# HGRN2 scores: lags 0 to 3 as elementwise products summed by a ones matrix, the tree from four up in place

## The chip, the cores and the metric

One NeuronCore of one Trainium2 chip runs the whole program. The metric is device time in microseconds, the median of several runs. Engines are named as in the profile: PE is TensorE (matmuls; PEld is its weight load), DVE is VectorE, ACT is ScalarE, POOL is GpSimd, SP is SyncE, which issues the DMAs.

## The reference

One layer of a hybrid decoder step for 256 prompt tokens and 8 x 8 sample tokens (320 in all), model width 2048, all in float32. One input projection feeds two mixers, an mLSTM branch (4 heads) and an HGRN2 branch (8 heads, key width 128, value width 256); their outputs are projected, gated, merged, projected again, and a feed-forward layer of width 8192 follows. What the change touches is the HGRN2 recurrence,

```python
# S_t = diag(f_t) S_{t-1} + (1 - f_t) i_t^T,   o_t = S_t^T q_t, chunkwise:
G = jnp.cumsum(lfc, axis=2)                             # log decay, per key channel
rel = G[:, :, :, None, :] - G[:, :, None, :, :]         # t, s, key
rel = jnp.where(causal[:, :, None], rel, -jnp.inf)
a = jnp.sum(qc[:, :, :, None, :] * jnp.exp(rel) * kc[:, :, None, :, :], axis=-1)
o = einsum('bhts,bhsv->bhtv', a, ic) + einsum('bhtk,bhkv->bhtv', qc * jnp.exp(G), S)
```

that is, a score a[t, s] for each pair s <= t: the sum over the 128 key channels of q_t, k_s and the product of the decays f between s and t. The decay depends on the channel, so the scores are not one matmul of q and k.

## The kernel before

The layout has features on the 128 partitions and the 320 tokens along the free dimension: 256 prompt tokens as two tiles of 128, then 64 sample tokens, eight sequences of eight.

**The stream of projections.** Nearly all matmul work is one stream of 304 output tiles of 128 features, each 16 contraction blocks deep, in the fixed order of `tile_list`. Operands are split into a high and a low fp32r part: ACT rounds the high part, DVE subtracts to get the low part, and three fp32r matmuls 320 wide (high x high, high x low, low x high) stand for one fp32 one. Weights come as half tiles of 128 x 1024 through three raw buffers (`wr`), and are split into three buffer pairs (`wh`, `wl`; `prep`, L465). Each head of HGRN2 follows four weight tiles: `hf`, `hq` and two `hi`, with two gate tiles ahead.

**Who sets the order.** While the program is built, a planner (`Sched`, with chains written as Python generators) keeps an estimated clock for each engine. After the matmuls of each contraction block it advances every side chain whose inputs it believes ready, and only then emits the instruction. So side work of a head is strewn between the projection matmuls, and each engine then executes its own instructions in that emitted order. Costs are given by `act`, `dve`, `pe_f` and `pe_r` and by pools of buffers (`acq`, `rel`); a side matmul is emitted once its input is 450 ns old by the planner's clock (`PE_LAT`) beyond a latency of 140.

**The scores of a head** are built as a tree in `h_scan` and `h_a`. At level B (1, 2, 4, ..., 64) tokens are taken in blocks of 2B; for pairs with s in the left half and t in the right half, the score is the dot product of (k_s times the decays from s to the end of its half) and (q_t times the decays from the start of its half to t). `h_scan` keeps these running factors in `fs` (left in one row, right in the other), multiplies them into q and k at each level (L1297, one product of 320 or 256 elements into a buffer `y`), and extends them by the other half's total (L1302 and L1304). `h_a` multiplies the tiles of `y` on PE in plain fp32, 64 columns for each of three (levels 1, 2, 4, with the sample tokens) or two tiles, and copies the pairs that belong to the level into the score buffer `at` under a mask (L1342). The diagonal is a matmul of q and k times the identity (L1327). Level 128, between the two prompt tiles, is one 128-wide matmul.

`h_state` and `h_update` handle the sample states, `h_sp` the prompt's final state, `h_i` the values, `h_out` the outputs. The masks are loaded at the program's start as int32 and narrowed by POOL.

Of the kernel before, what the change touches and what calls it, by code (L numbers as in the profile page):

```python
# [8 lines left out]
F32 = mybir.dt.float32  # L9
# [18 lines left out]
LEVELS = (1, 2, 4, 8, 16, 32, 64)  # L28
# [50 lines left out]
def constants():  # L79
# [16 lines left out]
    m = np.zeros((128, len(LEVELS), 64), np.int32)  # L96
    for n, b in enumerate(LEVELS):
        right = (i // b) % 2 == 1
        t = i[right]
        m[:, n, :] = (i[:, None] // (2 * b) == t[None, :] // (2 * b)) & ((i[:, None] // b) % 2 == 0)  # L100
# [6 lines left out]
    return c, m.reshape(128, -1), r.reshape(128, 256)  # L107
# [178 lines left out]
class Program:  # L286
    def __init__(self, tc, nc, d, pools):
# [3 lines left out]
        self.lmask = p.tile([128, len(LEVELS) * 64], U8, name="lmask")  # L291
# [12 lines left out]
        self.f2 = p.tile([128, 5280], F32, name="f2")  # L304
# [29 lines left out]
    def carve(self):  # L334
# [42 lines left out]
        self.at = Pool([A(512) for _ in range(2)])  # L377
        self.yb = Pool([A(384) for _ in range(2)])
# [7 lines left out]
        self.hkz0 = self.ra[:, 5376:6400]  # L386
        self.hkst = Pool([self.hkz0.rearrange("p (x g k) -> p x g k", x=4, g=2)])
# [4 lines left out]
        self.sg = Pool([Part(self.f2, 4960)(320), self.tst2])  # L392
# [8 lines left out]
    def carve_h(self):  # L401
        C = self.Part(self.pool.tile([128, 5120], F32, name="f3h", tag="f3"))
        qz = C(256)
        self.hqz = Pool([qz])
        for x in (qz, self.ats0, self.hkz0.bitcast(F32), *(y[64:128, 2, :] for y in self.it2)):
# [7 lines left out]
        self.sg.free += [(now, self.f2[:, 4960:5280]), (now, self.late[0])]  # L413
        self.sr.free.append((now, self.late[1]))
        self.ld = Pool(self.late[2:])
# [134 lines left out]
    def before(self, i, t):  # L550
# [44 lines left out]
    def start(self):  # L595
# [28 lines left out]
        lm = self.f2[:, 0:448].bitcast(I32)  # L624
        self.dma(lm, d["lmask"])
# [8 lines left out]
        nc.gpsimd.tensor_copy(self.lmask, lm)  # L634
# [579 lines left out]
    def h_start(self, h):  # L1214
# [4 lines left out]
        m["qk"], m["fs"], m["iv"] = a.three(2, 384), a.three(2, 320), a.three(2, 320)  # L1219
        for n in ("f", "q", "lv", "o", "pre8", "suf", "I", "SP", "S", "aT", "qz", "ist", "sdone", "got", "ld"):  # L1220
            m[n] = Ev()
        m["i"] = [Ev(), Ev()]
        m["Y"] = [Ev() for _ in range(9)]
        s = self.s
        s.spawn(self.h_scan(h), 4)
        s.spawn(self.h_a(h), 4)
# [21 lines left out]
    def ev_hf(self, h, c, b):  # L1248
        v, m = self.nc.vector, self.hh[h]
        fs, qk = m["fs"], m["qk"]  # L1250
        u = fs[:, 0, :]
        if h < 4:
            yield ("pool", 200, lambda: self.nc.gpsimd.memset(qk[:, :, 320:384], 0.0))
        yield from self.sigmoid(b[:, :TOK], u, fs[:, 1, :], ((self.mbank, b),))
        lb, l1 = self.lbv[:, h:h + 1], self.lbv[:, 8 + h:9 + h]
        yield ("dve", dve(TOK, mode=2), lambda: v.tensor_scalar(fs[:, 1, :], u, l1, lb, ALU.mult, ALU.add))
        yield ("act", act(TOK), lambda: self.A(qk[:, 0, 0:TOK], fs[:, 1, :], AF.Identity, scale=-1.0, bias=self.one))
        yield ("pool", 500, lambda: self.nc.gpsimd.memset(u, 1.0))
        yield post(m["f"])

    def ev_hq(self, h, c, b):
        m = self.hh[h]
        yield ("act", act(TOK, True), lambda: self.A(m["qk"][:, 1, 0:TOK], b[:, :TOK]))
        yield rel(self.mbank, b)
        yield post(m["q"])
# [17 lines left out]
    def h_scan(self, h):  # L1283

        v, m = self.nc.vector, self.hh[h]
        yield wait(m["f"], m["q"], m["got"])
        qk, fs = m["qk"], m["fs"]
        m["y"] = [None] * 9
        for n, B in enumerate(LEVELS + (128,)):
            T = TOK if B < 8 else NP_  # L1290
            y = yield acq(self.yb)
            pat = [[2 * B, T // (2 * B)], [320 + B, 2], [1, B]]
            patq = [[2 * B, T // (2 * B)], [384 + B, 2], [1, B]]
            if B < 8:
                yield ("pool", 150, lambda: self.nc.gpsimd.memset(y[:, 320:384], 0.0))
            yo = y[:, 0:T].rearrange("p (j c i) -> p j c i", c=2, i=B)
            yield ("dve", dve(T), lambda: v.tensor_tensor(yo, cap(qk, 0, patq), cap(fs, 0, pat), ALU.mult))  # L1297
            m["y"][n] = y
            yield post(m["Y"][n])
            half = lambda x, r: cap(fs, 320 * x + B * r, [[2 * B, T // (2 * B)], [1, B]])  # L1300
            tot = lambda r: cap(fs, 320 + B * r + B - 1, [[2 * B, T // (2 * B)], [0, B]])
            yield ("dve", dve(T / 2), lambda: v.tensor_tensor(half(0, 0), half(0, 0), tot(1), ALU.mult))  # L1302
            if B < 128:
                yield ("dve", dve(T / 2), lambda: v.tensor_tensor(half(1, 1), half(1, 1), tot(0), ALU.mult))  # L1304
            if B == 4:
                yield post(m["pre8"])
            if B == 128:

                yield post(m["suf"])

    def h_a(self, h):
        v, m = self.nc.vector, self.hh[h]
        if h:
            yield wait(self.hh[h - 1]["got"])
        yield wait(m["f"], m["q"])
        yield self.mdone()
        qk = m["qk"]
        at = yield acq(self.at)
        m["at"] = at
        yield post(m["got"])  # L1320
        a3 = at[:, 0:384].rearrange("p (a t) -> p a t", a=3)
        b = yield acq(self.sbank)
        for i in range(3):
            c = slice(128 * i, 128 * i + 128)
            yield ("pe", pe_f(128), lambda: self.mm(b[:, c], qk[:, 0, c], qk[:, 1, c], start=True, stop=True))
        idb = self.ident.unsqueeze(1).to_broadcast([128, 3, 128])
        yield ("dve", dve(384, True), lambda: v.tensor_tensor(a3, b[:, 0:384].rearrange("p (a t) -> p a t", a=3), idb, ALU.mult))  # L1327
        yield rel(self.sbank, b)
        for n, B in enumerate(LEVELS):
            yield wait(m["Y"][n])  # L1330
            y = m["y"][n]
            w = 3 if B < 8 else 2
            b = yield acq(self.sbank)
            for i in range(w):
                c = slice(128 * i, 128 * i + 128)
                right = y[:, c].rearrange("p (j c i) -> p j c i", c=2, i=B)[:, :, 1, :]
                yield ("pe", pe_f(64), lambda: self.mm(b[:, 64 * i:64 * i + 64], y[:, c], right, start=True, stop=True))
            yield rel(self.yb, y)
            ar = a3[:, 0:w, :].rearrange("p a (j c i) -> p a j c i", c=2, i=B)[:, :, :, 1, :]
            mk = self.lmask[:, 64 * n:64 * n + 64].unsqueeze(1).to_broadcast([128, w, 64]).rearrange("p a (j i) -> p a j i", i=B)  # L1340
            bv = b[:, 0:64 * w].rearrange("p (a j i) -> p a j i", a=w, i=B)
            yield ("dve", dve(64 * w, True) + (150 if w > 2 else 0), lambda: v.copy_predicated(ar, mk, bv))  # L1342
            yield rel(self.sbank, b)
        yield wait(m["Y"][7])
        y = m["y"][7]
        b = yield acq(self.sbank)
        yield ("pe", pe_f(128), lambda: self.mm(b[:, 0:128], y[:, 0:128], y[:, 128:256], start=True, stop=True))
        yield rel(self.yb, y)
        yield ("act", act(128, True), lambda: self.A(at[:, 384:512], b[:, 0:128]))
        yield rel(self.sbank, b)  # L1350
        yield post(m["aT"])

    def h_i(self, h):
# [17 lines left out]
        yield ("act", act(256, True), lambda: self.A(it[0:64, 2, :], b[64:128, 0:256]))  # L1371
# [30 lines left out]
    def h_state(self, h):  # L1402

        nc, v, m = self.nc, self.nc.vector, self.hh[h]
        if h:
            yield wait(self.hh[h - 1]["S"])
        yield wait(m["pre8"])
        qk, fs = m["qk"], m["fs"]

        qz = yield acq(self.hqz)  # L1410
        sv = lambda x: x[:, 256:320].rearrange("p (b t) -> p b t", t=8)
        yield ("dve", dve(64), lambda: v.tensor_tensor(
            cap(qz, 0, [[136, 2], [32, 4], [1, 8]]), by_token(qk[:, 1, :], 256, False), by_token(fs[:, 1, :], 256, False), ALU.mult))
        sm = yield acq(self.sm)
        yield ("dve", 80, lambda: v.tensor_copy(sm[:, 0:8], sv(fs[:, 1, :])[:, :, 7]))
        ks = fs[:, 0, 256:320]
        yield ("dve", dve(64), lambda: v.tensor_tensor(ks, qk[:, 0, 256:320], ks, ALU.mult))
# [20 lines left out]
        for g in range(2):  # L1438
            e = Ev()
            ends.append(e)  # L1440
            self.s.spawn(self.h_update(h, g, m["sb"][g], kst, sm, e), 5)
# [11 lines left out]
        yield rel(self.sm, sm)  # L1453
# [18 lines left out]
    def h_sp(self, h):  # L1472
# [5 lines left out]
        qk, fs, it = m["qk"], m["fs"], m["it"]  # L1478
        ks = fs[:, 0, 0:256]
        yield ("dve", dve(256), lambda: v.tensor_tensor(ks, qk[:, 0, 0:256], ks, ALU.mult))  # L1480
# [452 lines left out]
```

## Time and profile before

| | |
|---|---|
| median of 3 runs | 2347.54 us (2347.39 to 2348.0) |
| profiled execution, first to last instruction (span) | 2342.5 us; no other time of it is recorded, 5.0 us under the median of the runs |
| PE busy | 2331.8 us, 15956 matmul records |
| DVE, ACT, POOL busy | 1363.1, 1055.6, 15.6 us |
| HBM read, written | 371.57 MB, 50.90 MB |
| granted TensorE clock, mean | 0.998 |

A profile row names the line, the engine, the operation, output and input by the program's buffer names, the shape (partitions x elements) and a count; then busy time and the mean duration of one. A plain-fp32 matmul leaves two records, an fp32r one leaves one. Matmuls are pipelined and each record reaches into the next, so the busy column of PE is no price; differences between starts are.

### The profile page before, as it was taken

Reading aid. Unit: us, or ns where it says so; the run is one execution under the profiler, and the core shown is the slowest. Engines: PE = TensorE matmul, PEld = TensorE weight load, DVE = VectorE, ACT = ScalarE, POOL = GpSimd, SP = SyncE. Lnnn points to the kernel's source line nnn. Section 1 sums busy time; section 2 is a strip of 40 time slices with the busy share of each in tenths; the row PEclk is TensorE's granted clock in tenths of the full one; section 3 lists DMA queues with packets and bytes.
Section 4 is the critical chain, followed back from the end, with each engine's and each line's share of the span. In section 5 each row is a group of like instructions: output and inputs, shape, how many; then the busy total and the mean of one; then the engine's idle time right before and its main releaser. Section 6 shows DMA issues by size and latency. Waiting matters only on the chain.

```text
span 2342.5 us, 39167 instructions
## 1 busy us (share of the span) xinstructions
PE 2331.8 (100%) x15956; PEld 2289.7 (98%) x15956; DVE 1363.1 (58%) x2296; ACT 1055.6 (45%) x1685; POOL 15.6 (1%) x65
## 2 busy tenths in 40 slices
PE   9999999999999999999999999999999999999998
PEld 8999999999999999999999999999999999999998
DVE  5565566677666676555555766544554455445555
ACT  4444445445555565444433545533442344234434
POOL 0000000000000000000000000000000000000000
PEclk9999999999999999999999999999999999999999
DMA  7576857655554554545545644444444444444465
GB/s 247 195 259 209 285 189 271 231 182 209 171 180 171 178 188 169 181 170 175 176 168 177 222 166 144 145 152 152 145 147 151 152 145 152 146 153 144 153 225 180
DMA packets 145628, 425.03 MB, mean 181 GB/s; under 512 B 18468, under 2 KB 39972, under 8 KB 144424
## 3 DMA queue, kind: packets, MB, share of 16 engines
q1 hardware_dynamic: 143864, 415.72, 51.5%
q0 software_dynamic: 1152, 6.29, 0.8%
q8 instruction: 124, 2.03, 0.4%
q10 hardware_dynamic: 432, 0.52, 0.1%
q14 instruction: 56, 0.46, 0.1%
HBM read 371.57 MB, written 50.90 MB: 180 GB/s over the span
## 4 chain that ended last, share of the span: by engine, by line
PE 98%; DVE 1%; DMA 0%; ACT 0%; SPq 0%; issue 0%; DVEq 0%
PE bank L328 97%; DMA f<-xT 0%; DVE f3m L1827 0%; DVE f3m L1822 0%; PE bank L1534 0%; PE bank L917 0%; PE bank L1143 0%; PE bank L1365 0%; PE bank L1423 0%; PE bank L1370 0%; PE bank L990 0%; PE bank L1483 0%; PE bank L964 0%; DVE xl L673 0%; ACT xh L322 0%; SPq L331 0%
## 5 line engine op out<-in xcount | busy, mean ns | idle before, releaser
L465 DVE TENSOR_TENSOR wl<-wr,wh 128x1024 fp32r<-128x1024 f32 x428 | 524.4, 1225 | 477.4 <-ACT wh L322 473.4
L328 PE MATMUL bank<-xh,wh 128*128 128x320 f32 (+1 forms) x2432 | 794.8, 327 | 1.7 <-ACT xh L322 1.5
L328 PE MATMUL bank<-xh,wl 128*128 128x320 f32 (+1 forms) x2432 | 755.0, 310 | 0.0
L328 PE MATMUL bank<-xl,wh 128*128 128x320 f32 (+1 forms) x2432 | 753.6, 310 | 1.3 <-DVE xl L673 1.3
L322 ACT ACTIVATE wh<-wr 128x1024 fp32r<-128x1024 f32 (+1 forms) x431 | 453.7, 1053 | 436.6 <-PE bank L328 418.5
L328 PEld LDWEIGHTS bank<-xh,wh 128*128 128x128 f32 x2432 | 460.3, 189 | 20.5 <-issue 15.5
L328 PEld LDWEIGHTS bank<-xl,wh 128*128 128x128 f32 x2432 | 460.7, 189 | 4.7 <-DVE xl L673 1.9
L328 PEld LDWEIGHTS bank<-xh,wl 128*128 128x128 f32 x2432 | 459.4, 189 | 0.0
L465 DVE TENSOR_TENSOR bb<-wr,bb 128x1024 fp32r<-128x1024 f32 x179 | 219.4, 1226 | 236.1 <-ACT bb L322 236.1
L328 PE MATMUL bank<-xh,bb 128*128 128x322 f32 x1280 | 287.2, 311 | 0.0
L328 PE MATMUL bank<-ra,bb 128*128 128x320 f32 x1264 | 284.0, 309 | 0.0
L322 ACT ACTIVATE bb<-wr 128x1024 fp32r<-128x1024 f32 x179 | 188.8, 1055 | 208.2 <-PE bank L328 197.9
L328 PE MATMUL bank<-rxb,bb 128*128 128x320 f32 x1112 | 255.4, 310 | 0.0
L328 PE MATMUL bank<-ra,wh 128*128 128x320 f32 x892 | 250.2, 309 | 0.0
L328 PEld LDWEIGHTS bank<-xh,bb 128*128 128x128 f32 x1280 | 216.0, 188 | 0.0
L328 PEld LDWEIGHTS bank<-ra,bb 128*128 128x128 f32 x1264 | 210.7, 188 | 0.4
L328 PE MATMUL bank<-xl,bb 128*128 128x322 f32 x640 | 198.9, 311 | 0.0
L328 PEld LDWEIGHTS bank<-rxb,bb 128*128 128x128 f32 x1112 | 188.3, 188 | 0.2
L322 ACT ACTIVATE f<-f,misc 128x320 f32<-128x320 f32 x210 | 118.1, 562 | 148.9 <-DVE f L1790 137.2
L328 PE MATMUL bank<-rxb,wh 128*128 128x320 f32 x596 | 184.5, 310 | 0.0
L328 PE MATMUL bank<-rxb,wl 128*128 128x320 f32 x596 | 184.1, 309 | 0.0
L328 PEld LDWEIGHTS bank<-ra,wh 128*128 128x128 f32 x892 | 161.6, 188 | 1.1 <-DVE ra L1564 1.0
(246 smaller groups left out, 2274.2 us busy)
## 6 DMA issues: line engine op xcount, KB each, us to landing
wr<-wt SPq DMA_DIRECT2D x607, 512.0 KB, 3.3
rx<-C SPq DMA_DIRECT2D x34, 256.0 KB, 4.9
Cs<-rx SPq DMA_DIRECT2D x34, 256.0 KB, 4.4
f<-C SPq DMA_DIRECT2D x30, 256.0 KB, 5.0
Cs<-f SPq DMA_DIRECT2D x30, 256.0 KB, 4.4
vD<-ra SPq DMA_DIRECT2D x4, 1024.0 KB, 7.4
f<-S SPq DMA_DIRECT2D x8, 512.0 KB, 6.1
f3h<-S SPq DMA_DIRECT2D x8, 512.0 KB, 6.0
```

The source lines that it names most:

```text
L322: return self.nc.scalar.activation(out, in_, func, **kw)
L328: self.nc.tensor.matmul(*a, **kw)
L465: self.V().tensor_tensor(lo, raw, hi.bitcast(F32), ALU.subtract)
```

## The change

A head's scores are built in another way; everything else stays.

- **Lags 0 to 3** (s = t - d within a block of four tokens) no longer go through the tree. DVE multiplies q, shifted by d, with k into a buffer `P`: 320, 240, 160 and 80 products for d = 0, 1, 2, 3, that is 800 columns; between lags q is multiplied by the decay, so after the last one q holds its factor for the level of four. `P` is split into a high and a low fp32r part (ACT, then DVE), and PE sums over the 128 channels with a matrix of ones as the stationary operand: four fp32r matmuls, 480 and 320 wide for each part. Every row of the result then holds the sums, and masked copies put them on the diagonals of `at` (`h_lag`), which POOL has filled with zeros.
- **The tree begins at four** and works in place: k and q themselves carry the factors, the totals of the blocks lie in small buffers `t[2]` to `t[128]`, and there are no buffers `fs` and `y` and no products into them.
- **Levels 32 and 64** take both prompt tiles in one matmul 128 wide: ACT gathers the left halves of both tiles into a buffer `yk`, and small ACT copies place the blocks of the result into `at` (`h_put`). Levels 4, 8 and 16 stay with a matmul for each tile and a masked copy.
- `h_a` is gone; the placing runs in chains of its own (`put`). The next head's scan waits for this head's `sc`. The state chains read k and q directly (one DVE product for the sample queries becomes an ACT copy; two DVE products and a small copy go).
- The masks are bytes from the host, loaded when the first `mk` tile starts, without the narrowing by POOL. Some buffers move or shrink (`at` 512 to 496, `f2` 5280 to 5232).

```diff
-LEVELS = (1, 2, 4, 8, 16, 32, 64)
+LEVELS = (8, 16)
+M_LAG = (0, 320, 560, 720)
+M_4, M_8, M_END = 800, 960, 960 + 64 * len(LEVELS)
...
         elif kind == "mk" and h == 0 and c == 0:
             self.load_ev.t = s.t["pe"]
+            self.dma(self.lmask, self.d["lmask"])
...
     def h_scan(self, h):
-        yield wait(m["f"], m["q"], m["got"])
-        for n, B in enumerate(LEVELS + (128,)):
-            T = TOK if B < 8 else NP_
-            y = yield acq(self.yb)
...
-            yield ("dve", dve(T), lambda: v.tensor_tensor(yo, cap(qk, 0, patq), cap(fs, 0, pat), ALU.mult))
...
-            yield ("dve", dve(T / 2), lambda: v.tensor_tensor(half(0, 0), half(0, 0), tot(1), ALU.mult))
+        if h:
+            yield wait(self.hh[h - 1]["sc"])
+        yield wait(m["fd"], m["qd"])
+        k, q, f, t = m["k"], m["q"], m["f"], m["t"]
+        P = yield acq(self.pb)
...
+        for d in range(4):
+            n = 80 * (4 - d)
...
+            p = place(P, d).rearrange("p (b r) -> p b r", r=4 - d)
+            yield ("dve", dve(n), lambda: v.tensor_tensor(p, qr[:, :, d:4], kr[:, :, 0:4 - d], ALU.mult))
+            yield ("dve", dve(n), lambda: v.tensor_tensor(qr[:, :, d:4], qr[:, :, d:4], fr[:, :, 0:4 - d], ALU.mult))
...
+        yield ("act", act(800), lambda: self.A(ph, P))
...
+        yield ("dve", dve(800), lambda: v.tensor_tensor(pl, P, ph.bitcast(F32), ALU.subtract))
...
+        yield ("pool", 500, lambda: nc.gpsimd.memset(at[:, 0:TOK], 0.0))
+        ones = self.ones.bitcast(F32R)
+        b = yield acq(self.sbank, 2)
+        for i, (lo, hi) in enumerate(((0, 480), (480, 800))):
+            for x in range(2):
+                yield ("pe", pe_r(hi - lo), lambda: self.mm(b[i][:, 0:hi - lo], ones, phl[:, x, lo:hi], start=x == 0, stop=x == 1))
+        self.put(h, self.h_lag(b, at))
+        for B in (4, 8, 16, 32, 64, 128):
+            b = yield acq(self.sbank)
+            T = TOK if B == 4 else NP_
+            if B < 32:
+                for n, lo in enumerate((0, 128, 192) if B == 4 else (0, 128)):
+                    w = 32 if n == 2 else 64
...
+                    yield ("pe", pe_f(64), lambda: self.mm(b[:, 64 * n:64 * n + w], k[:, lo:lo + 128], right, start=True, stop=True))
+            elif B < 128:
+                yk = yield acq(self.hyk)
...
+                yield ("act", act(128), lambda: self.A(cap(yk, 0, [[64, 2], [32, 2], [1, 32]] if B == 32 else [[64, 2], [1, 64]]), left))
+                yield ("pe", pe_f(128), lambda: self.mm(b[:, 0:128], yk, right, start=True, stop=True))
+            else:
+                yield ("pe", pe_f(128), lambda: self.mm(b[:, 0:128], k[:, 0:128], q[:, 128:256], start=True, stop=True))
+            self.put(h, self.h_put(b, at, B))
...
+            yield ("dve", dve(T / 2), lambda: v.tensor_tensor(two(k)[:, :, 0, :], two(k)[:, :, 0, :], wide(1), ALU.mult))
             if B < 128:
+                yield ("dve", dve(T / 2), lambda: v.tensor_tensor(two(q)[:, :, 1, :], two(q)[:, :, 1, :], wide(0), ALU.mult))
+                yield ("dve", 90, lambda: v.tensor_tensor(t[2 * B][:, 0:T // (2 * B)], tt[:, :, 0], tt[:, :, 1], ALU.mult))
...
-    def h_a(self, h):
-            for i in range(w):
...
-                yield ("pe", pe_f(64), lambda: self.mm(b[:, 64 * i:64 * i + 64], y[:, c], right, start=True, stop=True))
...
+    def h_lag(self, b, at):
...
+        for d in (0, 2, 1, 3):
+            n = 80 * (4 - d)
...
+            yield ("dve", dve(n, True), lambda: v.copy_predicated(
+                a4[:, :, d:4], block(self.lmask[:, M_LAG[d]:M_LAG[d] + n]), block(x[:, lo:lo + n])))
...
+    def h_put(self, b, at, B):
+        if B == 128:
+            yield ("act", act(128, True), lambda: self.A(at[:, 368:496], b[:, 0:128]))
+        elif B >= 32:
+            for j in range(64 // B):
+                for i in range(2):
+                    lo, c = 64 * j + B * i, 128 * i + 64 * j
+                    yield ("act", act(B, True), lambda: self.A(
+                        at[64 * j:64 * j + B, c + B:c + 2 * B], b[lo:lo + B, c // 2:c // 2 + B]))
...
     def h_state(self, h):
-        yield ("dve", dve(64), lambda: v.tensor_tensor(
-            cap(qz, 0, [[136, 2], [32, 4], [1, 8]]), by_token(qk[:, 1, :], 256, False), by_token(fs[:, 1, :], 256, False), ALU.mult))
+        yield ("act", act(64), lambda: self.A(cap(qz, 0, [[136, 2], [32, 4], [1, 8]]), by_token(q, 256, False)))
```

How the order changes, on the two engines of the prediction. First PE while the first two heads run (bank_86 and bank_87 are their PSUM banks for scores; f_75 is the memory that holds a head's buffers; bank_83 belongs to a projection tile). Before, level matmuls 64 wide stand singly between the groups of three projection matmuls:

```order
L328 MATMUL bank_86<-f_75 128x64
L328 MATMUL bank_87<-f_75 128x64
L328 MATMUL bank_83<-xh,wh 128x320
L328 MATMUL bank_83<-xl,wh 128x320
L328 MATMUL bank_83<-xh,wl 128x320
L328 MATMUL bank_86<-f_75 128x64
```

And now, at the first head's sums over the channels (ra holds the split products, rh and ra in the last row are the sample values' spread):

```order
L336 MATMUL bank_88<-ra,ones 128x480
L336 MATMUL bank_82<-xh,wh 128x320
L336 MATMUL bank_82<-xl,wh 128x320
L336 MATMUL bank_82<-xh,wl 128x320
L336 MATMUL bank_82<-xh,wh 128x320
L336 MATMUL bank_82<-xl,wh 128x320
L336 MATMUL bank_82<-xh,wl 128x320
L336 MATMUL bank_88<-ra,ones 128x480
L336 MATMUL bank_82<-xh,wh 128x320
L336 MATMUL bank_82<-xl,wh 128x320
L336 MATMUL bank_82<-xh,wl 128x320
L336 MATMUL bank_85<-rh,ra 128x256
```

The projection matmuls keep their order and number; over the program 88 fp32 matmuls of the scores are gone and 32 fp32r ones against the ones have come. Second, DVE at a level of the tree, before (L1297 the product, L1342 the masked copy, L465 the subtraction that splits a weight half):

```order
L1302 TENSOR_TENSOR f_75<-f_75 128x80x2
L1304 TENSOR_TENSOR f_75<-f_75 128x80x2
L1297 TENSOR_TENSOR f_75<-f_75 128x320
L1342 COPY_PREDICATED f_75<-lmask,bank_88 128x192
L465 TENSOR_TENSOR wl<-wr,wh 128x1024
L1302 TENSOR_TENSOR f_75<-f_75 128x40x4
```

Now, where a head's lag products stand (L1305 and L1306, L475 is the weight split, L1253, L1254 and L1261 the sigmoid of a forget gate, L1518 a sample state's update):

```order
L475 TENSOR_TENSOR wl<-wr,wh 128x1024
L1354 TENSOR_TENSOR f_75<-f_75 128x128
L1306 TENSOR_TENSOR f_75<-f_75 128x80x3
L1518 SCALAR_TENSOR_TENSOR f_75<-f_75,bank_87 128x256
L1253 SCALAR_TENSOR_TENSOR f_75<-f_75 128x320
L1305 TENSOR_TENSOR f_75<-f_75 128x160
L1254 SCALAR_TENSOR_TENSOR f_75<-f_75 128x320
L1261 TENSOR_SCALAR f_75<-f_75,misc 128x320
L1306 TENSOR_TENSOR f_75<-f_75 128x80x2
L475 TENSOR_TENSOR wl<-wr,wh 128x1024
```

The lag products of one head lie among the tree's updates of the head before it, up to eight instructions between two weight splits.

More of the change, by code (lines that the diff above doesn't have):

```diff
@@ L290, in __init__ @@
         self.cst = p.tile([128, C_END], F32, name="cst")
-        self.lmask = p.tile([128, len(LEVELS) * 64], U8, name="lmask")
+        self.lmask = p.tile([128, M_END], U8, name="lmask")
         self.vec = p.tile([128, V_END], F32, name="vec")
@@ L303, in __init__ @@
         self.f1 = p.tile([128, 10240], F32, name="f1", tag="f1")
-        self.f2 = p.tile([128, 5280], F32, name="f2")
+        self.f2 = p.tile([128, 5232], F32, name="f2")
         self.f3 = p.tile([128, 5120], F32, name="f3", tag="f3")
@@ L376, in carve @@
         self.sb = Pool([A.three(4, 256) for _ in range(2)])
-        self.at = Pool([A(512) for _ in range(2)])
-        self.yb = Pool([A(384) for _ in range(2)])
+        self.at = Pool([A(496) for _ in range(2)])
+        self.pb = Pool([A(800)])
         self.ktk = Pool([A.three(2, 128)])
@@ L404, in carve_h @@
         self.hqz = Pool([qz])
-        for x in (qz, self.ats0, self.hkz0.bitcast(F32), *(y[64:128, 2, :] for y in self.it2)):
+        self.hyk = Pool([C(128)])
+        for x in (qz, self.ats0, self.hkz0.bitcast(F32), *(y[0:64, 2, :] for y in self.it2)):
             self.nc.gpsimd.memset(x, 0.0)
@@ L412, in carve_h @@
         self.sb.free += [(now, C.three(4, 256)) for _ in range(2)]
-        self.sg.free += [(now, self.f2[:, 4960:5280]), (now, self.late[0])]
+        self.sg.free += [(now, self.f2[:, 4912:5232]), (now, self.late[0])]
         self.sr.free.append((now, self.late[1]))
@@ new lines, in h_scan @@
+        if h:
[3 more added lines that the diff above has]
+        P = yield acq(self.pb)
+        four = lambda x: x.rearrange("p (b r) -> p b r", r=4)
+        kr, qr, fr = four(k), four(q), four(f)
+        place = lambda x, d: x[:, (0, 480, 320, 720)[d]:(320, 720, 480, 800)[d]]
+        for d in range(4):
+            n = 80 * (4 - d)
+            if d == 0:
+                yield ("dve", dve(n), lambda: v.tensor_tensor(place(P, 0), q, k, ALU.mult))
+                yield ("dve", dve(n), lambda: v.tensor_tensor(q, q, f, ALU.mult))
+                continue
+            p = place(P, d).rearrange("p (b r) -> p b r", r=4 - d)
+            yield ("dve", dve(n), lambda: v.tensor_tensor(p, qr[:, :, d:4], kr[:, :, 0:4 - d], ALU.mult))
+            yield ("dve", dve(n), lambda: v.tensor_tensor(qr[:, :, d:4], qr[:, :, d:4], fr[:, :, 0:4 - d], ALU.mult))
@@ new lines, in h_scan, with put, run @@
+        yield post(m["suf"])
+        yield wait(*m["Y"])
+        yield post(m["aT"])
+    def put(self, h, gen):
+        e = Ev()
+        self.hh[h]["Y"].append(e)
+        def run():
+            yield from gen
+            yield post(e)
+        self.s.spawn(run(), 4)
+    def h_lag(self, b, at):
+        v = self.nc.vector
+        a4 = at[:, 0:TOK].rearrange("p (b r) -> p b r", r=4)
+        for d in (0, 2, 1, 3):
+            n = 80 * (4 - d)
+            x = b[d % 2]
+            lo = (0, 0, 320, 240)[d]
+            block = lambda y: y.rearrange("p (b r) -> p b r", r=4 - d)
+            yield ("dve", dve(n, True), lambda: v.copy_predicated(
+                a4[:, :, d:4], block(self.lmask[:, M_LAG[d]:M_LAG[d] + n]), block(x[:, lo:lo + n])))
+            if d > 1:
+                yield rel(self.sbank, x)
@@ L1860 @@
     xT=(128, KT, TOK), wif=(128, KT, 8), wt=(len(UNITS), 128, 1024), vec=(128, V_END), m0=(MH, NB), n0=(128, 64),
-    C0=(MH, NB, 128, 1024), S0=(HH, 128, NB, HV), cst=(128, C_END), lmask=(128, len(LEVELS) * 64), spread=(128, 256),
+    C0=(MH, NB, 128, 1024), S0=(HH, 128, NB, HV), cst=(128, C_END), lmask=(128, M_END), spread=(128, 256),
 )
```

156 lines of the change are left out of this document (67 added, 89 removed).

## Prediction

> **What bounds the kernel now.** I read the page's busy row, its chain, the waits of TensorE, and then the stretch in which the heads of the HGRN2 branch run (480 to 830 us), in that order. The page:
>
> ```profile
> span 2342.5 us, 39167 instructions
> PE 2331.8 (100%) x15956; PEld 2289.7 (98%) x15956; DVE 1363.1 (58%) x2296; ACT 1055.6 (45%) x1685; POOL 15.6 (1%) x65
> PE 98%; DVE 1%; DMA 0%; ACT 0%; SPq 0%; issue 0%; DVEq 0%
> ```
>
> TensorE (PE) is busy for the whole span, and the chain that ended last is 98% PE. VectorE (DVE) and ScalarE (ACT) have room. The waits of PE alone:
>
> ```profile
> PE bank L328 <- ACT xh L322: 1.5, 1, 1.5
> PE bank L328 <- DVE xl L673: 1.3, 2, 0.9
> PE bank L328 <- POOL ones L601: 1.0, 1, 1.0
> ```
>
> These four waits, 3.8 us, all name the operands of the program's start; once it runs, PE waits for nobody. The heads' stretch (columns: PE, PEld, DVE, ACT, POOL busy, each with its instructions, then the granted clock, DMA share, GB/s):
>
> ```profile
> 480.00:830.00 350.00, 350.00 (x2544) 341.79 (x2543) 244.06 (x617) 186.75 (x391) 4.72 (x28) 1.00 0.53 178
> ```
>
> PE fills all 350 us at a granted clock of 1.00, DVE is at 70%, ACT at 53%. So a PE instruction taken out of this stretch shortens the program by what it occupies, as long as the others keep PE fed. The busy column cannot price it: records overlap. I price by start times, as the delay that an inserted matmul causes among the projection matmuls (128x320), which run without a break:
>
> ```profile
> 561.11 0.31 PE L328 MATMUL bank<-xh,wl 128*128 128x320 f32 x1
> ...
> 562.43 0.31 PE L328 MATMUL bank<-xh,wl 128*128 128x320 f32 x1
> ```
>
> Nine of them start in 1.32 us: 0.147 us each.
>
> **The change on PE.** Per head, before: 17 plain-fp32 matmuls 64 wide (three for each of the levels 1, 2, 4, two for each of 8, 16, 32, 64) and four 128 wide (three for the diagonal, one for level 128): 21. After: three for level 4 (one only 32 wide), two for 8, two for 16, one each 128 wide for 32, 64, 128: 10. New: four fp32r matmuls against the ones matrix, two 480 and two 320 wide. One 64-wide fp32 matmul is two records; two places of it, and one 128 wide:
>
> ```profile
> 566.47 0.31 PE L328 MATMUL bank<-xh,wl 128*128 128x320 f32 x1
> 566.61 0.33 PE L328 MATMUL bank<-f 128*128 128x64 f32 x2
> 566.75 0.39 PE L328 MATMUL bank<-xh,wh 128*128 128x320 f32 x1
> 566.98 0.31 PE L328 MATMUL bank<-xl,wh 128*128 128x320 f32 x1
> ...
> 564.22 0.31 PE L328 MATMUL bank<-xh,wl 128*128 128x320 f32 x1
> 564.37 0.33 PE L328 MATMUL bank<-f 128*128 128x64 f32 x2
> 564.51 0.40 PE L328 MATMUL bank<-xh,wh 128*128 128x320 f32 x1
> 564.75 0.31 PE L328 MATMUL bank<-xl,wh 128*128 128x320 f32 x1
> ...
> 579.13 0.31 PE L328 MATMUL bank<-xh,wl 128*128 128x320 f32 x1
> 579.27 0.39 PE L328 MATMUL bank<-f3h 128*128 128x128 f32 x2
> 579.41 0.39 PE L328 MATMUL bank<-xh,wh 128*128 128x320 f32 x1
> 579.64 0.31 PE L328 MATMUL bank<-xl,wh 128*128 128x320 f32 x1
> ```
>
> From the first row of each piece to its last are two projection matmuls (0.294) and the insert. 64 wide: 0.51 - 0.294 = 0.216 and 0.53 - 0.294 = 0.236; 128 wide: 0.51 - 0.294 = 0.216. So a plain-fp32 matmul costs 0.22 us whether it is 64 or 128 wide, and I book 0.22 for the 32-wide one too. Not one of the removed matmuls is cheaper for being narrow, and that is the whole of the gain: 21 - 10 = 11 fewer, x 0.22 x 8 heads = 19.4 us off PE (19.0 to 20.8 by the two ends).
>
> The ones matmuls have no row before. At 320 wide the fp32r projection matmul is the same thing: 0.147. For 480 the next wider one is
>
> ```profile
> 69.75 0.32 PE L328 MATMUL bank<-xh,wl 128*128 128x320 f32 x1
> 69.90 0.41 PE L328 MATMUL bank<-ra 128*128 128x512 f32 x1
> 70.15 0.31 PE L328 MATMUL bank<-xh,wh 128*128 128x320 f32 x1
> ```
>
> that is 0.40 - 0.147 = 0.25 at 512 wide. So 480 lies between 0.147 and 0.25, and I take 0.233, in proportion to the columns. Per head 2 x 0.147 + 2 x 0.233 = 0.76, x 8 = 6.1 us back on PE (4.7 to 6.4). Net -19.4 + 6.1 = **-13.3 us**; the ends give -12.6 to -16.1.
>
> Would it pay by the width? The Trainium skill says in "TensorE: Matmul & The Clock Gate", section "Step-by-step: what each phase is for", that a stream of matmuls costs its N cycles, one per moving column. By that rule half-wide matmuls would be half price, which the rows contradict (0.22 and 0.22); it is a rival below. The same page's section "LDWEIGHTS (loading the stationary operand)" gives 107 ns for loading 128 columns, whatever streams behind; at two loads for a matmul that would put the sum at about -12.7 us, an estimate by that page.
>
> **The change on the other engines**, which matters only if PE comes to wait. DVE rows of 430 to 880 us (instruction, count, busy, mean ns):
>
> ```profile
> L465 DVE TENSOR_TENSOR wl<-wr,wh 128x1024 fp32r<-128x1024 f32 x104 | 127.4, 1225 | 95.2 <-ACT wh L322 94.8
> L1297 DVE TENSOR_TENSOR f<-f 128x256 f32<-128x256 f32 x30 | 12.5, 420 | 0.7 <-PE bank L328 0.4
> L1342 DVE COPY_PREDICATED f<-lmask,bank 128x192 f32<-128x192 uint8 x24 | 12.3, 510 | 0.0
> L1302 DVE TENSOR_TENSOR f<-f 128x128 f32<-128x128 f32 x30 | 8.6, 288 | 0.3
> ```
>
> 128 elements take 288 ns, 256 take 420: 1.03 ns an element and 0.156 us an instruction. Before, a head has 35 DVE instructions of 6216 elements in scan, scores, state start and state product (8 products 2240, 15 updates 2112, 7 masked copies 1088, the diagonal 384, four others 392): 6.4 + 5.5 = 11.9 us. After, 36 of 5718: 8 lag products 1600, five for pairs and the low half 1360, 4 + 3 masked copies 1216, 11 updates 1472, 5 totals 70: 5.9 + 5.6 = 11.5 us. The masked copies with runs of one to three elements are the open price: 510 ns for 192 is 0.15 us above that line, so the four lag copies may cost up to 0.6 us more. DVE per head is unchanged within 0.6 us, under 2% of the some 44 us that a head has (350 / 8). It stays near 70%.
>
> ACT gains, per head, the rounding of 800 elements, two copies of 128, six more small copies out of PSUM, and one of 64:
>
> ```profile
> L322 ACT ACTIVATE wh<-wr 128x1024 fp32r<-128x1024 f32 x104 | 109.8, 1055 | 68.2 <-PE bank L328 62.6 <-issue 3.5 <-ACT rh L322 1.6
> L322 ACT ACTIVATE f<-f 128x320 f32<-128x320 f32 x28 | 12.8, 456 | 3.0 <-DVE f L1239 3.0
> L322 ACT ACTIVATE f<-f 128x64 f32<-128x64 f32 x8 | 2.0, 248 | 0.0
> ```
>
> 800 lies between 456 and 1055: 0.86 us; with nine small ones at 0.25 to 0.3, some 3.2 us a head, 7% of 44: ACT goes from 53% to about 60%. I book it at nothing, because ACT's weight roundings wait mostly for PE to free a buffer (62.6 of 68.2 us). What covers it: 24 projection matmuls use a weight half up in 24 x 0.147 = 3.53 us, there are three buffer pairs, so a half may be split any time in the two before it, 7.06 us, and its split takes 1.055 + 1.225 = 2.28 us. 4.8 us are spare. Without that cover each microsecond of lateness would be one of PE.
>
> POOL loses 28 small fills and a cast. SP issues the mask's load later (at the first key tile, about 0.4 us of queue time in front of one weight reload) and not between the start's loads:
>
> ```profile
> 15.04 0.43 SPq L331 DMA_DIRECT2D f<-lmask  x1
> ```
>
> PE waits for neither there; zero.
>
> **The sum.** Span 2342.5 - 13.3 = 2329.2. The median of the three runs, 2347.54, lies 5.0 above the span, and what lies around the span does not change: **2334.2 us**, 0.57% less. A measurement of this kernel can tell about 0.2% (4.7 us) from no change.
>
> **The rivals.**
>
> (a) Forecast: PE keeps running without a break. For it: the 3.8 us of waits above, DVE's load equal. Chance 0.82, 2332 to 2336.5.
>
> (b) PE comes to wait at the new joints. The ones matmuls stand behind a longer chain than a level did: eight products, ACT's rounding of 800, DVE's subtraction of 800, then PE in program order, with projection matmuls queued behind; levels 32 and 64 now wait for an ACT copy. The planner books 760 and 902 ns for the two long ones, my rows say 0.86 and 0.98 (0.156 + 800 x 1.03 ns), 0.2 us late. The cover is seen at a level of before: the product ends at 655.82, its matmul starts at 656.57.
>
> ```profile
> 655.40 0.42 DVE L1297 TENSOR_TENSOR f<-f 128x256 f32<-128x256 f32 x1
> 656.57 0.33 PE L328 MATMUL bank<-f 128*128 128x64 f32 x2
> ```
>
> 0.75 us of slack against 0.2. If the slack fails at three places a head by 0.25 us, 24 x 0.25 = 6 us come back: 2340. Chance 0.09.
>
> (c) PE is paid by the column, the skill's first rule above. Then a pass is 0.147 / 320 = 0.46 ns a column, a 64-wide fp32 matmul 2 x 0.029 = 0.059, a 128-wide 0.118. Before: 17 x 0.059 + 4 x 0.118 = 1.47 us a head; after: 6 x 0.059 + 0.029 + 3 x 0.118 + 1600 x 0.46 ns = 1.47. Nothing gained: 2347.5. Against it stand 0.216 and 0.216 at 64 and 128 wide. Chance 0.03.
>
> (d) Slower: the weight splits starve PE in the heads. The products of the lags and the 800-wide pair stand in DVE's one queue with the weight subtractions; between two of these the changed order holds up to eight instructions, about 3.3 us by the rows. The point is the 4.8 us spare: if bursts on ACT and DVE together pass it, PE stops. To end slower by 0.2% PE would have to lose 13.3 + 4.7 = 18 us, 2.25 us a head, a burst of 7 us in each. Time then 2352 or more. Against it: DVE's total load does not rise. Chance 0.04.
>
> The remaining 0.02 is spread. That the change fails to do what it says (the count of matmuls) is excluded by the order, which holds 88 fp32 matmuls fewer and 32 fp32r more.
>
> **How the numbers follow.** The likeliest case gives 2334.2. Its own bounds are 2331.4 to 2334.9, stretched by small waits to 2336.5; the range reaches up into (b), 2332 to 2341, leaving out (c), (d) and little else. Faster by over 0.2%: (a) and nearly all of (b), 0.91; within 0.2%: (c) and some of (b) and the rest, 0.05; slower: 0.04.
>
> **What would show it.** The page's PE row should read x15812 (15956 - 2 x 88 + 32), its waits still some 4 us, and a program position behind the heads should come 13 us earlier. A 64-wide insert should still cost 0.22, the 480-wide ones 0.22 to 0.25, ACT's 800 rounding 0.86 us, DVE's busy time in the heads' stretch 70%. I am wrong if PE shows waits on DVE or ACT at lines of the score code, if weight splits arrive late there, or if the ones matmuls cost well over 0.25 each.

## The result, and the profile after

The changed kernel takes 2334.41 us (median of 4 runs, 2332.48 to 2335.47), the kernel before on the same chip 2347.77 us (2347.39 to 2349.61). The ratio is 0.9942, with a 95% interval of 0.993 to 0.9954: 13.4 us less, where 2334.2 us and 13.3 us less had been forecast. In a later group of runs, the changed kernel again against before (e0_same) gave 2335.58 and 2347.22 us, ratio 0.9952 (0.9938 to 0.9966).

The page of the changed kernel, profiled in an execution of 2335.47 us, is shown in its span, busy row and shares of the chain:

```profile
span 2333.5 us, 38987 instructions
PE 2320.9 (99%) x15812; PEld 2276.1 (98%) x15812; DVE 1359.4 (58%) x2304; ACT 1074.2 (46%) x1765; POOL 11.5 (0%) x36
PE 97%; DMA 1%; DVE 1%; ACT 0%; issue 0%; SPq 0%; DVEq 0%; ACTq 0%
```

PE has 15812 records, the number forecast, and is still the engine that the end hangs on. The two spans differ by 9.0 us only, because the profiled execution of before was a quick one (see the steps below). So the change is better read within the program. The heads lie between the same two projection matmuls in both kernels: the first of the 55th tile of `tile_list` and the first of the 106th. Before:

```profile
462.23 0.31 PE L328 MATMUL bank<-xh,wh 128*128 128x320 f32 x1
...
905.79 0.30 PE L328 MATMUL bank<-xh,wh 128*128 128x320 f32 x1
```

And after:

```profile
464.52 0.30 PE L336 MATMUL bank<-xh,wh 128*128 128x320 f32 x1
...
895.17 0.30 PE L336 MATMUL bank<-xh,wh 128*128 128x320 f32 x1
```

905.79 - 462.23 = 443.56 us before, 895.17 - 464.52 = 430.65 after: **-12.91 us**. Three traces of before give 443.56, 443.59 and 443.59; two of the changed kernel give 430.65 each. The instructions that PE runs in this stretch are the same in both kernels but for the scores. No other stretch between matched matmuls differs steadily by more than 0.5 us: from the heads' end to the 161st tile the changed kernel takes 0.20 more, in the tail 0.5 more (why was not tried). So the steady gain of the program is about 12.2 us. What is left scatters alike in both kernels; counted from the program's start, the matmul behind the heads comes 10.6 us earlier in these two traces, because the changed kernel's reached the heads 2.3 us later.

What PE waited for in the changed kernel (line, releaser: us in total, times, longest):

```profile
PE bank L336 <- ACT xh L330: 2.2, 1, 2.2
PE bank L336 <- DVE xl L681: 1.3, 2, 0.9
PE bank L336 <- POOL ones L612: 1.0, 1, 1.0
PE bank L336 <- DVE f L1708: 0.8, 1, 0.8
PE bank L336 <- ACT f L330: 0.2, 1, 0.2
```

The first three are the program's start, as before. L1708 is in a layer normalization near 1315 us, and the last lies near 370 us, ahead of the heads. They are 5.5 us in all, and in the heads themselves PE waits for nobody. Busy time there, before (first row) and after (PE, PEld, DVE, ACT, POOL, each with its instructions; clock; DMA share; GB/s):

```profile
462.00:906.00 444.00, 444.00 (x3192) 435.55 (x3191) 307.12 (x730) 239.25 (x483) 7.52 (x38) 1.00 0.53 182
```

```profile
464.00:895.00 431.00, 431.00 (x3047) 421.17 (x3046) 299.71 (x727) 257.02 (x561) 4.66 (x13) 1.00 0.57 188
```

DVE stays at 70% (299.71 / 431, before 69%), and ACT goes from 54% to 60%, as forecast.

### The profile page after: what moved, and what is told of

Its sections match the earlier page's. It is cut to its first block, busy times and chain, and to the rows that moved or that the text cites. A ratio compares the mean times of both kernels' runs of the same rounds, so it can differ in the third digit from the quotient of the medians.

```text
span 2333.5 us, 38987 instructions
## 1 busy us (share of the span) xinstructions
PE 2320.9 (99%) x15812; PEld 2276.1 (98%) x15812; DVE 1359.4 (58%) x2304; ACT 1074.2 (46%) x1765; POOL 11.5 (0%) x36
## 4 chain that ended last, share of the span: by engine, by line
PE 97%; DMA 1%; DVE 1%; ACT 0%; issue 0%; SPq 0%; DVEq 0%; ACTq 0%
PE bank L336 95%; DMA wr<-wt 1%; DMA f<-xT 0%; DVE f3m L1874 0%; DVE f3m L1879 0%; PE bank L925 0%; PE bank L1586 0%; DMA gaD<-f 0%; PE bank L1151 0%; PE bank L1424 0%; DVE bb L475 0%; ACT wh L330 0%; ACT bb L330 0%; DVE wl L475 0%; ACT f L330 0%
## 5 line engine op out<-in xcount | busy, mean ns | idle before, releaser
L475 DVE TENSOR_TENSOR wl<-wr,wh 128x1024 fp32r<-128x1024 f32 x428 | 524.3, 1225 | 476.8 <-ACT wh L330 471.0
L475 DVE TENSOR_TENSOR bb<-wr,bb 128x1024 fp32r<-128x1024 f32 x179 | 219.3, 1225 | 236.5 <-ACT bb L330 236.4
```

The lines of the kernel that those rows point to most:

```text
L475: self.V().tensor_tensor(lo, raw, hi.bitcast(F32), ALU.subtract)
```

## The experiments

Diffs are against the changed kernel, unless said otherwise. "Heads" is the time between the two matmuls above in the experiment's own trace, to set against 430.65. `...` marks lines left out.

**e0_same**: the changed kernel again, as the mate of the others.

> The changed kernel once more, nothing edited: what its time and its profile scatter by. Theory A (the gain is 11 fp32 matmuls less per head, less the four ones matmuls; PE never waits in the heads): 2332.5 to 2335.5 us, and from the first head's tiles to the last the profile is again 12.5 to 13.3 us shorter than before; the start (0.9 us longer in the first profile of the change) and single late loads scatter by about 1 us each. Theory B (the later load of the masks makes the start or the mLSTM part slower): the 0.9 us at the start and the 1.3 us around 370 to 430 us come again in the same places.

Measured 2335.58 us (2334.33 to 2336.28), heads 430.65 to the hundredth. The heads' stretch is a ruler good to a few hundredths, while whole times scatter by 2 to 3 us.

**e1_wide**: levels 4, 8 and 16 multiply the whole tile of queries, not the right halves alone, so 56 fp32 matmuls have twice the moving columns. The masked copies pick out the halves.

```diff
-w = 32 if n == 2 else 64
...
+w = 64 if n == 2 else 128
...
-yield ("pe", pe_f(64), lambda: self.mm(b[:, 64 * n:64 * n + w], k[:, lo:lo + 128], right, start=True, stop=True))
+yield ("pe", pe_f(64), lambda: self.mm(b[:, 128 * n:128 * n + w], k[:, lo:lo + 128], q[:, 128 * n:128 * n + w], start=True, stop=True))
...
```

> The seven matmuls of levels 4, 8 and 16 take all columns of a tile (128, and 64 for the sample tokens) where they took the right halves (64 and 32); the copies read the same columns as before, the scores are the same. Theory A (a plain-fp32 matmul up to 128 columns is priced by its two weight loads): no change to within 1 us. Theory C (PE is paid by the column, 0.46 ns a column and record): 416 columns more per head in two records, 0.38 us a head, 3.1 us slower.

Measured 2333.87 us (2333.6 to 2336.62), ratio to before 0.995 (0.9937 to 0.9962). Heads 430.99: +0.34 us for 56 matmuls twice as wide, 6 ns each. By the column, 416 columns a head more, in two passes of 0.46 ns, would have been 8 x 416 x 2 x 0.46 ns = 3.1 us. Rival (c) falls. Here the trace does not agree with the rule of N cycles for a stream (the Trainium skill, "TensorE: Matmul & The Clock Gate", section "Step-by-step: what each phase is for"): up to 128 columns the width of a plain-fp32 matmul among others costs next to nothing.

**e2_twice**: each of these 56 matmuls is issued twice.

```diff
+for _ in range(2):
     yield ("pe", pe_f(64), lambda: self.mm(b[:, 64 * n:64 * n + w], k[:, lo:lo + 128], right, start=True, stop=True))
```

> Each of the seven matmuls of levels 4, 8 and 16 is issued twice into the same place, 56 plain-fp32 matmuls more in the program. Theory A: 56 x 0.22 = 12.3 us slower, about the whole gain given back (2346.7). Theory C (by the column): 8 x 0.38 = 3.1 us slower. Theory D (PE has hidden room in the heads): no change.

Measured 2346.48 us (2345.12 to 2348.83), ratio 0.9998 (0.9989 to 1.0006). The count gives nearly the whole gain back. The bounding matmuls:

```profile
465.50 0.30 PE L336 MATMUL bank<-xh,wh 128*128 128x320 f32 x1
...
907.69 0.30 PE L336 MATMUL bank<-xh,wh 128*128 128x320 f32 x1
```

442.19 us, +11.54 for 56 matmuls. But this stretch does not hold the same work as the changed kernel's: six transpositions of a head's outputs, which there lie ahead of its end, now come behind it (907.69).

```profile
L1587 PE MATMUL bank<-cst,f x6: 270/272/272, 915.6 to 924.5; 128*128 128x128 f32 x6
```

The stretch up to the first matmul of the 161st tile holds them in both programs. That matmul comes here at

```profile
1295.70 0.31 PE L336 MATMUL bank<-rxb,wh 128*128 128x320 f32 x1
```

and in the changed kernel at

```profile
1282.45 0.31 PE L336 MATMUL bank<-rxb,wh 128*128 128x320 f32 x1
```

that is (1295.70 - 465.50) - (1282.45 - 464.52) = 12.27 us for 56: **0.219 us each**. In e1, e3, e4, e5, e8 and e9 the heads hold the changed kernel's work but for the edit, so there the shorter stretch serves. Together e1 and e2 say that what is paid is the matmul, not its columns.

**e3_apart**: levels 32 and 64 go back to one matmul for each prompt tile (16 more over the program), without the gathering ACT copy.

```diff
-            if B < 32:
+            if B < 128:
...
```

> Levels 32 and 64 take each prompt tile by itself again: two matmuls 64 wide for each level and no gathering copy on ACT; the small placing copies stay. Two plain-fp32 matmuls more per head. Theory A: 16 x 0.22 = 3.5 us slower. Theory C (by the column): the columns are the same, no change. Theory B2 (the gathering copies hold PE up): no change or faster.

Measured 2337.44 us (2335.86 to 2339.51), ratio 0.9963 (0.9949 to 0.9976).

```profile
465.37 0.30 PE L336 MATMUL bank<-xh,wh 128*128 128x320 f32 x1
...
899.36 0.30 PE L336 MATMUL bank<-xh,wh 128*128 128x320 f32 x1
```

Heads 433.99, +3.34 us for 16 matmuls: 0.209 each, nearly the same price from another part of the change. So taking both tiles at once is worth 3.3 of the 12.9 us, and the ACT copies in front of it cost PE nothing.

**e4_high**: the two ones matmuls of the low part are left out, so the scores of lags 0 to 3 have only their high part.

```diff
-for x in range(2):
-    yield ("pe", pe_r(hi - lo), lambda: self.mm(b[i][:, 0:hi - lo], ones, phl[:, x, lo:hi], start=x == 0, stop=x == 1))
+yield ("pe", pe_r(hi - lo), lambda: self.mm(b[i][:, 0:hi - lo], ones, phl[:, 0, lo:hi], start=True, stop=True))
```

> The ones matmuls of the low parts are left out (16 in the program: the lags are summed from the rounded products alone, so this part of the computation is missing); ACT and DVE do what they did. Theory A: 8 x (0.233 + 0.147) = 3.0 us faster. Theory E (the ones matmuls cost little because the same weights are loaded again and again): under 1 us faster.

Measured 2330.98 us (2330.35 to 2333.67), ratio 0.9936 (0.9924 to 0.9949).

```profile
462.65 0.30 PE L336 MATMUL bank<-xh,wh 128*128 128x320 f32 x1
...
890.37 0.30 PE L336 MATMUL bank<-xh,wh 128*128 128x320 f32 x1
```

Heads 427.72, -2.93 us for one 480-wide and one 320-wide matmul a head: 0.366 for the pair. All four a head so cost 5.9 us over the program, against 6.1 forecast.

**e5_plain**: the sums over the channels as two plain-fp32 matmuls against the ones, without the split into high and low.

```diff
-yield ("act", act(800), lambda: self.A(ph, P))
-yield ("dve", dve(800), lambda: v.tensor_tensor(pl, P, ph.bitcast(F32), ALU.subtract))
...
-for x in range(2):
-    yield ("pe", pe_r(hi - lo), lambda: self.mm(b[i][:, 0:hi - lo], ones, phl[:, x, lo:hi], start=x == 0, stop=x == 1))
+yield ("pe", pe_f(hi - lo), lambda: self.mm(b[i][:, 0:hi - lo], self.ones, P[:, lo:hi], start=True, stop=True))
```

> The lag products are summed in plain fp32, two ones matmuls of 480 and 320 columns, without the split (no rounding of 800 on ACT, no subtraction of 800 on DVE). Theory A: above 128 columns plain fp32 goes by the columns; by the 0.21 us of a record at 256 columns a record takes 0.40 at 480 and 0.27 at 320, so 1.34 us for the two where the four took 0.75: 8 x 0.59 = 4.7 us slower. Theory B (the long chain in front of the ones matmuls holds PE up): at most that, or faster. If two weight loads priced them at any width (0.22 each), 2.5 us faster.

Measured 2338.82 us (2337.84 to 2341.26), ratio 0.9969 (0.9958 to 0.998), heads 435.53: +4.88 us, 0.61 a head. One place of a 320-wide one:

```profile
473.85 0.31 PE L336 MATMUL bank<-xh,wl 128*128 128x320 f32 x1
474.00 0.70 PE L336 MATMUL bank<-f,ones 128*128 128x320 f32 x2
474.29 0.55 PE L336 MATMUL bank<-xh,wh 128*128 128x320 f32 x1
474.68 0.31 PE L336 MATMUL bank<-xl,wh 128*128 128x320 f32 x1
```

474.68 - 473.85 - 0.294 = 0.54 us, against 2 x 0.147 for the two fp32r ones. The pair of widths costs 0.61 + 0.366 x 2 = 1.34 us a head (0.366 by e4), which leaves 0.80 for the 480-wide one: 0.80 to 0.54 is nearly 480 to 320, so at these widths plain fp32 is paid by the column. So the split pays for itself, since ACT and DVE have room.

**e8_thrice**: DVE's 800-wide subtraction is done three times, 2 x 0.98 us a head more in the burst of rival (d).

```diff
+for _ in range(3):
     yield ("dve", dve(800), lambda: v.tensor_tensor(pl, P, ph.bitcast(F32), ALU.subtract))
```

> The subtraction of 800 on DVE is issued three times (the same result): 16 more, 15.7 us of DVE time in the heads, in bursts of 3 us in the one queue with the weight splits. Theory A: DVE is covered (it is busy 70% of that stretch and a weight split has 4.8 us to spare): no change to within 1 us. Theory D2 (DVE's bursts starve PE): 5 to 15 us slower.

Measured 2335.05 us (2332.98 to 2337.6), ratio 0.9953 (0.9941 to 0.9966). Heads 430.69, +0.04. The 16 more subtractions sum to 15.7 us (23.6 us for 24, against 7.9 for 8), and DVE's busy time on the page is 12.6 us more:

```profile
PE 2321.2 (99%) x15812; PEld 2276.2 (98%) x15812; DVE 1372.0 (59%) x2320; ACT 1074.1 (46%) x1765; POOL 11.5 (0%) x36
```

None of it reaches PE, although this DVE queue also carries the weight splits. Rival (d) falls, with some 2 us a head to spare at the least.

**e7_early**: the planner's margin between an operand and the side matmul that reads it goes from 450 ns to nothing, for all side work of the program.

```diff
-PE_LAT = 450.0
+PE_LAT = 0.0
```

> The planner's wait before it emits a side matmul (450 ns beyond the latency) is set to 0 for the whole program: side matmuls stand earlier in PE's order, with that much less cover. Theory A (in the change the joints have room to spare because of this cover): PE comes to wait for DVE and ACT in the heads and before them, the program gets slower by some 5 to 30 us. Theory B (the cover is not what keeps PE running): no change to within 1 us.

Measured 2337.67 us (2335.43 to 2339.49), ratio 0.9958 (0.9945 to 0.9972); e0_same has 0.9952 (0.9938 to 0.9966), and the two cannot be told apart. The setting moved side work to earlier places (17 us more in the 40 tiles from the third on, 9.5 less in the heads), so the heads' stretch cannot be compared here. PE's longest waits:

```profile
PE bank L972 <- DVE np_o L965: 1.9, 2, 1.4
PE bank L336 <- DVE f L1708: 1.7, 1, 1.7
PE bank L336 <- DVE xl L681: 1.5, 2, 1.0
```

Theory A's 5 to 30 us did not come, and B's 1 us was not quite held: 2.1 us over e0_same by the medians, within the scatter. None of the three waits is at a line of the score code. I had taken the planner's margin for the cover of the new joints, but without it PE still waits for nobody there. Nor does all slack go with it: by the starts and ends in the two traces, the least time between ACT's gathering copy and the matmul that reads it falls from 0.42 to 0.19 us, and between DVE's 800-wide subtraction and the ones matmul that reads it from 2.15 to 1.85 us.

**e9_from1**: the tree in place from level one, with the diagonal as three matmuls: no lag products, no ones matmuls.

```diff
-for d in range(4):
...
+t[1] = f
...
-        yield ("pe", pe_r(hi - lo), lambda: self.mm(b[i][:, 0:hi - lo], ones, phl[:, x, lo:hi], start=x == 0, stop=x == 1))
+    yield ("pe", pe_f(128), lambda: self.mm(b[:, 128 * n:128 * n + w], k[:, lo:lo + 128], q[:, 128 * n:128 * n + w], start=True, stop=True))
...
-for B in (4, 8, 16, 32, 64, 128):
+for B in (1, 2, 4, 8, 16, 32, 64, 128):
```

> The tree begins at one again, still in place: the diagonal is three matmuls of k and q, levels 1 and 2 are three each, placed by masked copies; no lag products, no splitting, no ones matmuls. Per head nine plain-fp32 matmuls come and the four ones matmuls go. Theory A: 8 x (9 x 0.22 - 0.75) = 9.8 us slower than the change (2344.3). Theory C (by the column): 8 x (0.30 + 6 x 0.059 - 0.75) = about 1 us faster or nothing.

Measured 2343.77 us (2342.01 to 2345.75), ratio 0.9987 (0.9979 to 0.9996).

```profile
465.20 0.30 PE L336 MATMUL bank<-xh,wh 128*128 128x320 f32 x1
...
905.99 0.30 PE L336 MATMUL bank<-xh,wh 128*128 128x320 f32 x1
```

Heads 440.79, +10.14: that is what the lags are worth. With the 3.34 us of e3 it makes 13.5, near the 12.91 of the whole change; the two parts overlap little, if at all. By the 5.9 us that e4 gives for the ones matmuls, the 72 fp32 matmuls that came cost (10.14 + 5.9) / 72 = 0.222 us each. Its page has DVE at 1336.3 us, 23 less than the changed kernel, and that buys nothing: DVE is not what the time hangs on.

**e10_before, e11_before, e12_masks**: the first pair of traces showed 0.9 us more at the start of the changed kernel and 1.4 us more in the last tiles ahead of the heads. Two more single profiles of before, and the changed kernel with its masks loaded at the program's start as before, were to tell whether the masks' new place did that.

```diff
 elif kind == "mk" and h == 0 and c == 0:
-    self.dma(self.lmask, self.d["lmask"])
...
+        self.dma(self.lmask, d["lmask"])
```

> The kernel before, unchanged, for a second profile of it. Theory A: the heads' stretch takes 443.6 us again, to within 0.1; the stretch before it (the last mLSTM states, 97.8 us in the first profile, 99.2 to 100.9 with the change) scatters by its loads, and here too lies at 98 to 101 us. Theory B (the change makes that stretch longer): 97.8 again.

> The kernel before, unchanged, for a third profile of it; expected as for the second.

> The change, but the masks (bytes) are loaded at the program's start, between the same loads as before. Theory A: no change to within 1 us; the stretch of the last mLSTM states scatters as in the others. Theory B (the moved load delays the state loads): that stretch is back at 97.8 us and the time 1 to 2 us less than the change's.

Before gave 2345.76 and 2350.84 us, with 97.87 and 101.07 us in the 12 tiles ahead of the heads (97.83 in the first trace). e11_before waited there once for a state's load:

```profile
PE bank L328 <- DMA rx<-C: 2.0, 1, 2.0
```

The changed kernel has 99.19 and 100.88, and with the masks at the start 98.89: 2333.93 us (2332.5 to 2337.31), ratio 0.9948 (0.9936 to 0.9961). The masks' place makes no difference that these runs can show, and the 1.4 us lie within the scatter that both kernels have there: e5_plain, with the masks in the new place, has 97.91. In part that scatter is waits for a state's load, as in e11_before; for the 1.4 us of the first trace no wait above 0.2 us is named.

A version that computes everything and beats the changed kernel did not come out of this. e4_high is quicker by leaving out part of the sums, and e1_wide cannot be told from e0_same.

## Why the prediction was right, step by step

- **What bounds it.** PE, and a matmul taken out shortens the program by what it occupies. Shown: e2, e3 and e4 add or take away matmuls, and the time follows at 0.219, 0.209 and 0.183 us each.
- **The fp32 matmuls, 88 x 0.22 = 19.4 us.** At the upper end of what the runs give: 0.219 (e2), 0.209 (e3) and 0.222 (e9), that is 18.4 to 19.5 us. The price read off three rows was right for a matmul that stands alone: in the trace of before, the 80 places where a 64-wide one stands alone among projection matmuls delay them by 0.224 us in the mean. Where it stands beside a transposition of other work, the two together delay by 0.29 us (median of 23 places), while a transposition alone takes 0.114; there the matmul itself adds some 0.18. The forecast took one price for all places. That the width does not matter was right (e1). By the Trainium skill ("TensorE: Matmul & The Clock Gate", section "LDWEIGHTS (loading the stationary operand)") a load of 128 columns takes 107 ns, so two make 0.214, an estimate that agrees with these runs to 0.01; the sum by it, -12.7, lies nearer to the measured -12.91 than the forecast's -13.3, on its other side.
- **The ones matmuls, 6.1 us.** 5.9 by e4. In the trace of the changed kernel a 480-wide one delays its neighbours by 478.07 - 477.71 - 0.147 = 0.21 us, where 0.233 had been taken:

```profile
477.71 0.31 PE L336 MATMUL bank<-xh,wl 128*128 128x320 f32 x1
477.85 0.38 PE L336 MATMUL bank<-ra,ones 128*128 128x480 f32 x1
478.07 0.31 PE L336 MATMUL bank<-xh,wh 128*128 128x320 f32 x1
```

- **The net, -13.3.** -12.91 in the heads; the prices above make 12.5 to 13.6 of it, so the measured figure lies within them. Behind the heads 0.7 us are lost again, which the forecast did not have, so the steady gain is 12.2. The two groups of runs gave 13.4 and 11.6 us: that the first of them meets the forecast to 0.2 us is in part luck.
- **DVE unchanged within 0.6 us a head, ACT 0.86 and DVE 0.98 us for the 800-wide pair.** Right: DVE 1363.1 to 1359.4 us over the program, and these rows (430 to 870 us):

```profile
L330 ACT ACTIVATE ra<-f 128x800 fp32r<-128x800 f32 x8 | 6.9, 863 | 3.3 <-DVE f L1305 3.3
L1318 DVE TENSOR_TENSOR ra<-f,ra 128x800 fp32r<-128x800 f32 x8 | 7.9, 984 | 0.0
```

ACT rose by 18.6 us in all, 2.3 a head instead of 3.2.
- **Rival (b), PE waits at the new joints.** None in the heads. The 0.75 us of slack had been read at a level of before; at the long chain of the first head the subtraction ends at 475.28 + 0.98 = 476.26, and the second ones matmul, the first that reads its result, starts 2.70 us later:

```profile
475.28 0.98 DVE L1318 TENSOR_TENSOR ra<-f,ra 128x800 fp32r<-128x800 f32 x1
478.96 0.39 PE L336 MATMUL bank<-ra,ones 128*128 128x480 f32 x1
```

In the eight heads it is 2.15 to 2.92 us. At ACT's gathering copies it is 0.42 to 2.04. e7 says that less margin costs no more than the scatter.
- **The masks' load at nothing.** Right (e12).
- **The 5.0 us around the span: the step that failed.** It was the difference between the span of one execution and the median of others. Every run with both figures has 1.7 to 3.1 us between them, most about 2.0: 2335.47 against a span of 2333.5 here, 2345.76 against 2343.7 in e10_before. So the profiled execution of before probably took some 2344.5 us, 3 us less than the median of the runs shown. The prediction took the 5.0 us for what lies around the span and does not change; by the other runs only about 2.0 of it is that. It did no harm, because the gain was subtracted from a span and the 5.0 us carried that execution back to the median.

## What to carry to other kernels

Where a matmul stream bounds a kernel, price an insertion by the delay between its neighbours' starts, and count instructions before columns: narrow plain-fp32 matmuls are worth merging, or replacing by fewer wide fp32r ones, as long as the other engines' room pays for the preparation. To measure a gain of half a per cent, take the time between the same two instructions in both traces, which here held to 0.03 us where whole times scattered by 2 to 3; and count the instructions between them first, because a planner may have moved other work across the end (in e2 six transpositions, 0.7 us). Compare a span with spans and a median with medians.

## What the hardware showed unexpectedly

A plain-fp32 matmul has a floor, then a slope: 0.21 to 0.22 us at 64 columns (e2, e3, e9), 6 ns more at twice the width (e1), 0.54 us at 320 (e5). And a masked copy out of PSUM in short runs did not get cheaper with fewer elements (DVE, 430 to 870 us of the changed kernel):

```profile
L1383 DVE COPY_PREDICATED f<-lmask,bank 128x80 f32<-128x80 uint8 x8 | 4.2, 521 | 0.3
L1383 DVE COPY_PREDICATED f<-lmask,bank 128x320 f32<-128x320 uint8 x8 | 4.1, 518 | 0.1
L1383 DVE COPY_PREDICATED f<-lmask,bank 128x160 f32<-128x160 uint8 x8 | 4.1, 515 | 0.1
L1404 DVE COPY_PREDICATED f<-lmask,bank 128x160 f32<-128x160 uint8 x8 | 2.6, 326 | 0.0
```

L1383 copies a lag: 80 elements in runs of one and 320 in runs of four both take 0.52 us; each has 80 runs. L1404 copies 160 in 40 runs of four, and takes 0.33 us. Whether the price goes by the runs was not tried.
